# State-space groups of a two-block transformer: decay matrices a chunk ahead, row transposes a group later

## The chip, the core and the metric

The kernel runs on one core of one Trainium2 chip. The metric is the time of one execution in device microseconds. Five engines work side by side and meet at semaphores: TensorE (PE in the rows, its weight loads PEld), VectorE (DVE), ScalarE (ACT), GpSimd (POOL) and SyncE (SP, which here only issues DMAs). Each takes its own instructions in a fixed order.

## The reference, cut to what matters

A sequence of 512 tokens of width 1024 goes through a first block (window attention, indexed attention, cross attention, a feed-forward part) and a second block of two mixers: a state-space mixer and a latent attention. All is float32. The change lies in the state-space mixer alone:

```python
xbc = silu(causal_depthwise_conv(xbc, conv_w, conv_b))      # 4 taps; B, C and x of 8 groups
dt  = softplus(dt_raw + dt_bias);  a = dt * -exp(A_log)     # 32 heads, 4 in a group
# for each group g and each chunk c of 128 tokens:
cb       = C_c @ B_c.T                                      # (t, s)
decay_in = exp(where(causal, acum[t] - acum[s], -inf))      # one matrix for each head
y_diag   = (cb * decay_in) @ (x_c * dt)
y_off    = exp(acum) * (C_c @ state)                        # the state that enters the chunk
state    = exp(acum[-1]) * state + B_c.T @ (decay_to_end * dt * x_c)
y        = y_diag + y_off + D * x
y        = y * silu(z);  y = y * rsqrt(mean(y*y over the group's 256 columns) + eps)
out      = (y * norm_w) @ out_w
```

## The kernel before

Every product of the model is a float32 product made of three matmuls: each operand is split in a rounded part H and a rest L, and `mm3` (L127 to L131) adds H·H, H·L and L·H in PSUM. A weight tile of 128 by 1024 comes by a DMA on SP's queue, ACT makes H from it (L121), POOL makes L (L124). The program is written as plain Python and put in order by a planner: it keeps the order of the source as priority, places each instruction on its engine when its plan says that the inputs are there, and fills in later work where earlier work would wait. The order on each engine is fixed by that plan; on the chip an engine then waits at each instruction for its semaphores.

The state-space part is `block2a`. A PSUM bank holds 128 by 512 numbers; there are eight, three called mm, three px, one py, one po in this part (L1094). For each group g of 8:

- `proj(g, i)`, i = 0 to 3, is a product of 24 matmuls of 512 columns in an mm bank, and `conv` behind it: ACT writes the scaled last tap to `xbc` (L946), DVE adds three taps from PSUM (L948), ACT takes a tanh into the tile `th` (L950), DVE makes silu of both (L951).
- `gate(g, tp)`, tp = 0 and 1, is a product of 48 matmuls of 256 columns in an mm bank, a tanh (L973) and a product (L974).
- `prep(g)` splits B and C, makes C·B for four chunks (L992, px, then `cbm` by L994), transposes B (L997, px) and x (L1004, px twice), and makes `X`, `W` and `y0` (L1011 to L1018).
- `core(g, c)`, c = 0 to 3, has in this order: the decay matrix `Dm` (a DMA from the tensor `acd` issued on ACT's queue, L1028; relu and exp on ACT, L1030 and L1031; times `cbm` on DVE, L1032; split into `M`, L145 and L146), the state's split `E` and its product in po (L1040), the chunk's product in py (L1045 and L1046), the new state's product in px (L1050) and its sum (L1053 to L1056), `y` from py and po (L1062 to L1067), its norm (square on ACT L1070, a scale on DVE L1071, the power -0.5 on POOL L95, a scaled copy on ACT L1073).
- `tr`, one for each chunk, transposes the finished rows of y (L1078, px) and copies or splits them (L1082 to L1091). For g from 4 to 6 a DMA carries them on.

The loop at L1116 runs, for g = 0 to 7: proj 0 and 1 of group g+1, core 0, proj 2 and 3, core 1, gate 1 of group g, core 2, core 3, tr 0, prep of g+1, gate 0 of g+1, tr 1, 2, 3. For g = 7 there is no next group; the output product over Y (L1152) follows, and the planner may draw its first matmuls ahead. `split_first` and `split_second` (L1102 to L1113) make Y from the rows of groups 0 to 3 and 4 to 6.

Of the kernel before, what the change touches and what calls it, by code (L numbers as in the profile page):

```python
# [7 lines left out]
F32 = mybir.dt.float32  # L8
F32R = mybir.dt.float32r
AF = mybir.ActivationFunctionType  # L10
ALU = mybir.AluOpType
# [13 lines left out]
class Net:  # L25
# [891 lines left out]
    def block2a(self, dbg):  # L917
# [25 lines left out]
        def conv(g, i, ps):  # L943
            m = 4 * g + i
            o = gp.tile([P, T], F32, tag="xbc", name=self.nm("xbc"), bufs=5)
            nc.scalar.activation(o, ps, AF.Identity, bias=cb[:, m:m + 1], scale=cw[:, m, 3:4])  # L946
            for j in range(1, 4):
                nc.vector.scalar_tensor_tensor(o[:, j:], ps[:, :T - j], cw[:, m, 3 - j:4 - j], o[:, j:], op0=ALU.mult, op1=ALU.add)  # L948
            th = gp.tile([P, T], F32, tag="th", name=self.nm("th"), bufs=1)
            nc.scalar.activation(th, o, AF.Tanh)  # L950
            nc.vector.scalar_tensor_tensor(o, th, 1.0, o, op0=ALU.add, op1=ALU.mult)  # L951
            G[g]["xbc"].append(o)

        def proj(g, i):
# [23 lines left out]
        def prep(g):  # L978
# [11 lines left out]
            for c in range(NT):  # L990
                q = slice(c * P, (c + 1) * P)
                self.mm3(ps[:, q], BT[0][:, q], BT[1][:, q], CT[0][:, q], CT[1][:, q], c == 0, c == 3)  # L992
            cbm = d["cbm"] = gp.tile([P, NT, P], F32, tag="cbm", name=self.nm("cbm"), bufs=2)
            nc.vector.tensor_tensor(cbm, ps.rearrange("p (c t) -> p c t", t=P), tri.unsqueeze(1).to_broadcast([P, NT, P]), op=ALU.mult)  # L994
            ps = self.bank("px")
            for c in range(3):
# [17 lines left out]
            W = d["W"] = self.pair(gp, [P, 3, 256], "W", bufs=1)  # L1014
            nc.gpsimd.tensor_tensor(v4(xw[:, 0:3, :]), v4(xk[:, 0:3, :]), bc(wde, 3), op=ALU.mult)
            self.split(W[0], W[1], xw[:, 0:3, :])
            y0 = d["y0"] = gp.tile([P, NT, 256], F32, tag="y0", name=self.nm("y0"), bufs=1)
            nc.gpsimd.tensor_tensor(v4(y0), v4(xk), dsk.unsqueeze(1).unsqueeze(3).to_broadcast([P, NT, 4, 64]), op=ALU.mult)  # L1018

        def core(g, c):  # L1020
            d = G[g]
            XX, W, CT, Bt = d["X"], d["W"], d["CT"], d["Bt"]
            hs = slice(4 * g, 4 * g + 4)
            q = slice(c * P, (c + 1) * P)
            ch = lambda v: v[:, c, hs].unsqueeze(2).to_broadcast([P, 4, 64])

            Dm = gp.tile([P, 4, P], F32, tag="Dm", name=self.nm("Dm"), bufs=3)
            nc.scalar.dma_start(Dm, acd[c * 32 + 4 * g:c * 32 + 4 * g + 4, :].partition_broadcast(P))  # L1028
            for h in range(4):
                nc.scalar.activation(Dm[:, h, :], Dm[:, h, :], AF.Relu, bias=acum[:, c, 4 * g + h:4 * g + h + 1], scale=-1.0)  # L1030
            nc.scalar.activation(Dm, Dm, AF.Exp, scale=-1.0)  # L1031
            nc.vector.tensor_tensor(Dm, Dm, d["cbm"][:, c, :].unsqueeze(1).to_broadcast([P, 4, P]), op=ALU.mult)  # L1032
            M = self.pair(gp, [P, 4, P], "M", bufs=2)
            self.split(M[0], M[1], Dm)
            py = self.bank("py")
            if c:
                E = self.pair(gp, [P, 256], "E", bufs=2)
                self.split(E[0], E[1], d["st"])
                po = self.bank("po")[:, :256]
                self.mm3(po, CT[0][:, q], CT[1][:, q], E[0], E[1], True, True)  # L1040

            for h in range(4):
# [3 lines left out]
                nc.tensor.matmul(o[:, 0:64], M[1][:, h, :], XX[:, c, 0, dd], start=False, stop=True, skip_group_check=True)  # L1046

            if c < NT - 1:
                pst = self.bank("px")
                self.mm3(pst[:, :256], Bt[0][:, q], Bt[1][:, q], W[0][:, c, :], W[1][:, c, :], True, True)  # L1050
                sn = gp.tile([P, 256], F32, tag="st", name=self.nm("st"), bufs=2)
                if c == 0:
                    nc.vector.tensor_copy(sn, pst[:, :256])  # L1053
                else:
                    nc.gpsimd.tensor_tensor(w4(sn), w4(d["st"]), ch(dec), op=ALU.mult)
                    nc.vector.tensor_tensor(sn, pst[:, :256], sn, op=ALU.add)  # L1056
                d["st"] = sn

            y = d["y0"][:, c, :]
# [5 lines left out]
                nc.vector.tensor_tensor(w4(yo), w4(po), ch(ea), op=ALU.mult)  # L1065
                nc.gpsimd.tensor_tensor(y, y, yo, op=ALU.add)
            nc.gpsimd.tensor_tensor(y, y, d["zs"][c // 2][:, c % 2, :], op=ALU.mult)  # L1067
            ss = gp.tile([P, 1], F32, tag="gss", name=self.nm("gss"), bufs=4)
            sqj = gp.tile([P, 256], F32, tag="yo", name=self.nm("sqj"), bufs=1)
            nc.scalar.activation(sqj, y, AF.Square, accum_out=ss)  # L1070
            nc.vector.tensor_scalar(ss, ss, 1.0 / 256, 4e-6, op0=ALU.mult, op1=ALU.add)  # L1071
            self.rsq(ss, 1)
            nc.scalar.activation(y, y, AF.Copy, scale=ss)  # L1073

            def tr():
                pt = self.bank("px")
# [14 lines left out]
                    nc.sync.dma_start(dst, ys)  # L1091
            d[f"tr{c}"] = tr

        self.banks(mm=3, px=3, py=1, po=1)  # L1094
        self.ssm_dt(gp, G[0]["zs"], dt, acum, ea, wde, dec, tri, acd)
        for i, ps in enumerate(self.pre):
            conv(0, i, ps)
# [15 lines left out]
                self.split(*Y[k], yT[1][:, k - 8, :], scale=nwg[:, k:k + 1])  # L1113


        for g in range(8):  # L1116
            if g == 7:
                gate(7, 1)
                split_first()
                split_second()  # L1120
            proj(g + 1, 0)
            proj(g + 1, 1)
            core(g, 0)
            proj(g + 1, 2)
            proj(g + 1, 3)
            core(g, 1)
            if g < 7:
                gate(g, 1)
            core(g, 2)
            core(g, 3)  # L1130
            G[g]["tr0"]()
            prep(g + 1)
            gate(g + 1, 0)
            G[g]["tr1"]()
            G[g]["tr2"]()
            G[g]["tr3"]()
        self.flush()
        ctx.close()
        self.Rc = self.rcc.enter_context(self.pool("Rc", "right"))
# [45 lines left out]
    def ssm_dt(self, gp, zs, dt, acum, ea, wde, dec, tri, acd):  # L1185
        nc, a, u = self.nc, self.a, self.u

        scr = gp.tile([P, NT, 256], F32, tag="y0", name=self.nm("dts"), bufs=1).rearrange("p t c -> p (t c)")
        sl = [scr[:, x * P:(x + 1) * P] for x in range(8)]
        t3 = lambda x: x.rearrange("p (t h) -> p t h", h=32)  # L1190
        db, na = sl[7][:, 0:32], sl[7][:, 32:64]
        nc.scalar.dma_start(db, a["ssm_dt_bias"].partition_broadcast(P))
        nc.scalar.dma_start(na, a["ssm_A_log"].partition_broadcast(P))
        bc = lambda v: v.unsqueeze(1).to_broadcast([P, NT, 32])
        nc.scalar.activation(na, na, AF.Exp)
        nc.vector.tensor_scalar_mul(na, na, -1.0)
        v, e, z, z2, q = [t3(x) for x in sl[:5]]
        self.ssm_gate0(gp, v, db, zs)

        nc.vector.scalar_tensor_tensor(e, v, -1.0, v, op0=ALU.mult, op1=ALU.min)  # L1200
        nc.scalar.activation(e, e, AF.Exp)
        nc.vector.tensor_scalar_add(z, e, 2.0)
        nc.vector.reciprocal(z, z)
        nc.vector.tensor_tensor(z, z, e, op=ALU.mult)
        nc.vector.tensor_tensor(z2, z, z, op=ALU.mult)
        nc.vector.tensor_scalar_mul(q, z2, 1.0 / 17)
        for k in range(7, 0, -1):
            nc.vector.scalar_tensor_tensor(q, q, 1.0 / (2 * k + 1), z2, op0=ALU.add, op1=ALU.mult)
        nc.vector.scalar_tensor_tensor(q, q, 1.0, z, op0=ALU.add, op1=ALU.mult)
        nc.vector.tensor_scalar_max(v, v, 0.0)  # L1210
        nc.vector.scalar_tensor_tensor(dt, q, 2.0, v, op0=ALU.mult, op1=ALU.add)
        nc.vector.tensor_tensor(v, dt, bc(na), op=ALU.mult)
        self.defer(lambda: self.ssm_cum(sl, v, dt, acum, ea, wde, dec, tri, acd))
# [410 lines left out]
```

## Time and profile before

| | us |
|---|---|
| median of 3 runs | 1729.89 (1728.51 to 1731.52) |
| the profiled execution | 1732.23 |
| its span, first to last instruction | 1730.5 |

The state-space loop takes the stretch from about 880 to 1222 us of the span. In the profile's rows an engine's busy time is the union of its instructions; a matmul's end is modelled, so idle time of PE is read as a lower bound. "[2.35 <-DVE gss L1071]" behind an instruction says that its engine sat idle for 2.35 us before it, and whose semaphore came last. [...]

### The profile page before, as it was taken

How to read it: one execution, taken by the hardware profiler on the slowest of the kernel's cores; microseconds unless marked ns; L12 is line 12 of the kernel's file. 1: busy time of each engine (PE TensorE's matmuls, PEld its weight loads, DVE VectorE, ACT ScalarE, POOL GpSimd, SP SyncE). 2: the span in 40 equal slices, each digit the busy share in tenths (PEclk: the TensorE clock that was granted, in tenths of full speed). 3: DMA queues.
4: the chain of work that ended last, by engine and by line, in shares of the span. 5: the costliest groups of instructions: out<-in, count | busy, mean ns of one | idle time of the engine just before them, and what ended most of it. 6: DMA issues, size and time to landing. Idle time of an engine off the chain costs nothing.

```text
span 1730.5 us, 27236 instructions
## 1 busy us (share of the span) xinstructions
PE 1663.9 (96%) x10203; PEld 1479.8 (86%) x10203; DVE 927.3 (54%) x1981; ACT 834.1 (48%) x1694; POOL 907.9 (52%) x833
## 2 busy tenths in 40 slices
PE   6999999999999999999999899998999999999998
PEld 6877889889988888887978788888999888989898
DVE  7579763742653014303778877779321306667522
ACT  4455663453443123313557767767433326565532
POOL 6746434353375445544558777777634544344431
PEclk9999999999999999999999999999999999999999
DMA  7634313232232222222332222332324332122341
GB/s 282 196 107 130 106 48 143 95 110 86 86 120 87 97 99 88 95 98 95 125 117 92 86 86 98 110 101 95 146 98 155 130 123 76 52 75 92 110 141 50
DMA packets 68181, 187.23 MB, mean 108 GB/s; under 512 B 9968, under 2 KB 16544, under 8 KB 67792
## 3 DMA queue, kind: packets, MB, share of 16 engines
q1 hardware_dynamic: 50128, 152.95, 26.0%
q10 hardware_dynamic: 17632, 30.43, 5.5%
q8 instruction: 80, 1.31, 0.3%
q0 software_dynamic: 288, 2.10, 0.3%
q14 instruction: 53, 0.43, 0.1%
HBM read 163.86 MB, written 14.78 MB: 103 GB/s over the span
## 4 chain that ended last, share of the span: by engine, by line
PE 71%; DVE 14%; ACT 5%; issue 4%; DMA 3%; POOL 3%; ACTq 0%; DVEq 0%; SPq 0%; POOLq 0%
PE mm L129 12%; PE mm L131 12%; PE mm L130 12%; PE acc L129 5%; PE acc L130 5%; PE acc L131 5%; PE sc L130 2%; PE sc L131 2%; PE sc L129 2%; DMA Dm<-acd 2%; DVE xbc L948 2%; POOL wl L124 2%; PE pv L130 2%; PE pv L131 1%; PE pv L129 1%
## 5 line engine op out<-in xcount | busy, mean ns | idle before, releaser
L124 POOL TENSOR_TENSOR wl<-wraw,wh 128x512 fp32r<-128x512 f32 (+1 forms) x498 | 665.3, 1360 | 515.5 <-ACT wh L121 492.7
L121 ACT ACTIVATE wh<-wraw 128x1024 fp32r<-128x1024 f32 (+4 forms) x254 | 258.3, 1019 | 404.0 <-PE acc L131 123.7
L129 PE MATMUL mm<-xaH,wh 128*128 128x512 f32 x552 | 221.3, 401 | 1.8 <-DVE qbL L140 1.1
L131 PE MATMUL mm<-xaH,wl 128*128 128x512 f32 x552 | 220.8, 400 | 0.0
L130 PE MATMUL mm<-xaL,wh 128*128 128x512 f32 x552 | 220.5, 399 | 0.0
L129 PE MATMUL mm<-wh,xaH 128*128 128x256 f32 x512 | 145.1, 284 | 1.4 <-ACT xaH L145 1.4
L131 PE MATMUL mm<-wh,xaL 128*128 128x256 f32 x512 | 144.6, 284 | 0.9 <-DVE xaL L143 0.9
L130 PE MATMUL mm<-wl,xaH 128*128 128x256 f32 x512 | 144.2, 282 | 0.0
L129 PEld LDWEIGHTS mm<-xaH,wh 128*128 128x128 f32 x552 | 104.9, 190 | 26.1 <-DVE qbL L140 1.5
L131 PEld LDWEIGHTS mm<-xaH,wl 128*128 128x128 f32 x552 | 104.8, 190 | 24.5
L130 PEld LDWEIGHTS mm<-xaL,wh 128*128 128x128 f32 x552 | 104.9, 190 | 23.9
L878 POOL TENSOR_SCALAR S<-S,den 128x128 f32<-128x128 f32 (+1 forms) x96 | 50.9, 534 | 103.2 <-DVE den L877 88.2
L129 PEld LDWEIGHTS mm<-wh,xaH 128*128 128x128 f32 x512 | 96.4, 188 | 2.0 <-ACT xaH L145 1.8
L131 PEld LDWEIGHTS mm<-wh,xaL 128*128 128x128 f32 x512 | 96.2, 188 | 1.2 <-DVE xaL L143 1.1
L131 PE MATMUL mm<-wh,xbL 128*128 128x256 f32 x336 | 94.5, 284 | 2.4 <-DVE xbL L143 2.3
L130 PEld LDWEIGHTS mm<-wl,xaH 128*128 128x128 f32 x512 | 96.4, 188 | 0.2
L129 PE MATMUL mm<-wh,xbH 128*128 128x256 f32 x336 | 95.4, 285 | 0.7 <-DVE lnsum L256 0.5
L130 PE MATMUL mm<-wl,xbH 128*128 128x256 f32 x336 | 94.4, 282 | 0.0
L698 DVE TENSOR_TENSOR rl<-rl 128x512 f32<-128x512 f32 x32 | 43.7, 1365 | 78.5 <-ACT rl L697 78.5
L948 DVE SCALAR_TENSOR_TENSOR xbc<-mm,conv_w,xbc 128x511 f32<-128x511 f32 (+2 forms) x84 | 62.2, 742 | 18.2 <-ACT xbc L946 17.3
L131 PEld LDWEIGHTS mm<-wh,xbL 128*128 128x128 f32 x336 | 63.0, 189 | 3.5 <-DVE xbL L143 2.9
L876 ACT ACTIVATE S<-S,mx 128x128 f32<-128x128 f32 (+1 forms) x96 | 53.7, 560 | 22.6 <-DVE mx L875 20.8
(631 smaller groups left out, 4782.3 us busy)
## 6 DMA issues: line engine op xcount, KB each, us to landing
wraw<-in_w_up SPq DMA_DIRECT2D x32, 512.0 KB, 3.2
wraw<-in_w_down SPq DMA_DIRECT2D x32, 512.0 KB, 3.2
wraw<-in_ssm_xbc SPq DMA_DIRECT2D x32, 512.0 KB, 3.2
Dm<-acd ACTq DMA_DIRECT2D x32, 256.0 KB, 3.3
wraw<-in_ssm_out SPq DMA_DIRECT2D x16, 512.0 KB, 3.5
wraw<-in_mla_z SPq DMA_DIRECT2D x16, 512.0 KB, 3.4
wraw<-in_mla_out SPq DMA_DIRECT2D x16, 512.0 KB, 3.5
wraw<-in_ssm_z SPq DMA_DIRECT2D x14, 512.0 KB, 3.3
```

The costliest lines, as they stand in the source:

```text
L121: nc.scalar.activation(h[:, :n], raw[:, :n], AF.Copy)
L124: (leng or nc.gpsimd).tensor_tensor(l[:, e], raw[:, e], f32(h[:, e]), op=ALU.subtract)
L129: mm(out, aH, bH, start=first, stop=False, skip_group_check=True)
L130: mm(out, aH, bL, start=False, stop=False, skip_group_check=True)
L131: mm(out, aL, bH, start=False, stop=last, skip_group_check=True)
L698: nc.vector.tensor_tensor(r, r, r, op=ALU.mult)
L876: nc.scalar.activation(s, s, AF.Exp, bias=mx, scale=-1.0, accum_out=den)
L878: nc.gpsimd.tensor_scalar(s, s, den, 1.0, op0=ALU.mult, op1=ALU.mult)
L948: nc.vector.scalar_tensor_tensor(o[:, j:], ps[:, :T - j], cw[:, m, 3 - j:4 - j], o[:, j:], op0=ALU.mult, op1=ALU.add)
```

## The change

- `conv`: the tanh is written back into the mm bank that held the product, not into a tile of SBUF; L951 reads it there.
- `core` is cut in two: `decay(g, c)` has the decay matrix up to `M`, and `core(g, c)` the rest. decay 0 of a group is put ahead of proj 0, decay 1 ahead of proj 1, decay 2 behind core 0, decay 3 behind core 1.
- The rows of group g are transposed during group g+1 (two behind proj 0, two behind proj 1), those of group 7 after the loop.
- proj 3 stands between core 2 and core 3; gate 0 of the next group stands ahead of its prep. In group 7 `split_second` stands behind the transposes of group 6.
- py has two banks and px two, not three; the new state's product goes into the second half of the po bank, not into a px bank.
- The norm's scale and power are taken for two chunks at once, behind the odd one.
- `cbm` has one buffer, not two; `y0` has two, not one.

```diff
             nc.scalar.activation(o, ps, AF.Identity, bias=cb[:, m:m + 1], scale=cw[:, m, 3:4])
             ...
-            th = gp.tile([P, T], F32, tag="th", name=self.nm("th"), bufs=1)
-            nc.scalar.activation(th, o, AF.Tanh)
-            nc.vector.scalar_tensor_tensor(o, th, 1.0, o, op0=ALU.add, op1=ALU.mult)
+            nc.scalar.activation(ps, o, AF.Tanh)
+            nc.vector.scalar_tensor_tensor(o, ps, 1.0, o, op0=ALU.add, op1=ALU.mult)
...
-            cbm = d["cbm"] = gp.tile([P, NT, P], F32, tag="cbm", name=self.nm("cbm"), bufs=2)
+            cbm = d["cbm"] = gp.tile([P, NT, P], F32, tag="cbm", name=self.nm("cbm"), bufs=1)
...
-            y0 = d["y0"] = gp.tile([P, NT, 256], F32, tag="y0", name=self.nm("y0"), bufs=1)
+            y0 = d["y0"] = gp.tile([P, NT, 256], F32, tag="y0", name=self.nm("y0"), bufs=2)
...
-        def core(g, c):
+        def decay(g, c):
             d = G[g]
...
-            M = self.pair(gp, [P, 4, P], "M", bufs=2)
+            M = d["M", c] = self.pair(gp, [P, 4, P], "M", bufs=2)
             self.split(M[0], M[1], Dm)
+
+        def core(g, c):
+            d = G[g]
+            XX, W, CT, Bt, M = d["X"], d["W"], d["CT"], d["Bt"], d["M", c]
...
             py = self.bank("py")
+            ob = self.bank("po")
             if c:
                 E = self.pair(gp, [P, 256], "E", bufs=2)
                 self.split(E[0], E[1], d["st"])
-                po = self.bank("po")[:, :256]
+                po = ob[:, :256]
...
             if c < NT - 1:
-                pst = self.bank("px")
-                self.mm3(pst[:, :256], Bt[0][:, q], Bt[1][:, q], W[0][:, c, :], W[1][:, c, :], True, True)
+                pst = ob[:, 256:]
+                self.mm3(pst, Bt[0][:, q], Bt[1][:, q], W[0][:, c, :], W[1][:, c, :], True, True)
...
-            ss = gp.tile([P, 1], F32, tag="gss", name=self.nm("gss"), bufs=4)
+            if c % 2 == 0:
+                d["ss"] = gp.tile([P, 2], F32, tag="gss", name=self.nm("gss"), bufs=4)
+            ss = d["ss"]
             sqj = gp.tile([P, 256], F32, tag="yo", name=self.nm("sqj"), bufs=1)
-            nc.scalar.activation(sqj, y, AF.Square, accum_out=ss)
-            nc.vector.tensor_scalar(ss, ss, 1.0 / 256, 4e-6, op0=ALU.mult, op1=ALU.add)
-            self.rsq(ss, 1)
-            nc.scalar.activation(y, y, AF.Copy, scale=ss)
+            nc.scalar.activation(sqj, y, AF.Square, accum_out=ss[:, c % 2:c % 2 + 1])
+            if c % 2:
+                nc.vector.tensor_scalar(ss, ss, 1.0 / 256, 4e-6, op0=ALU.mult, op1=ALU.add)
+                self.rsq(ss, 2)
+                for i in range(2):
+                    yc = d["y0"][:, c - 1 + i, :]
+                    nc.scalar.activation(yc, yc, AF.Copy, scale=ss[:, i:i + 1])
...
-        self.banks(mm=3, px=3, py=1, po=1)
+        self.banks(mm=3, px=2, py=2, po=1)
...
         for g in range(8):
+            tr = [G[g - 1][f"tr{c}"] for c in range(NT)] if g else [lambda: None] * NT
+            decay(g, 0)
             if g == 7:
                 gate(7, 1)
                 split_first()
+            proj(g + 1, 0)
+            tr[0]()
+            tr[1]()
+            decay(g, 1)
+            proj(g + 1, 1)
+            tr[2]()
+            tr[3]()
+            if g == 7:
                 split_second()
-            proj(g + 1, 0)
-            proj(g + 1, 1)
             core(g, 0)
+            decay(g, 2)
             proj(g + 1, 2)
-            proj(g + 1, 3)
             core(g, 1)
+            decay(g, 3)
             if g < 7:
                 gate(g, 1)
             core(g, 2)
+            proj(g + 1, 3)
             core(g, 3)
-            G[g]["tr0"]()
+            gate(g + 1, 0)
             prep(g + 1)
-            gate(g + 1, 0)
-            G[g]["tr1"]()
-            G[g]["tr2"]()
-            G[g]["tr3"]()
+        for c in range(NT):
+            G[7][f"tr{c}"]()
```

## Rows read from the trace of the kernel before

**Rows 1.** The page's first part: PE's busy time, share of the span, instructions.
```profile
PE 1663.9 (96%) x10203; PEld 1479.8 (86%) x10203; DVE 927.3 (54%) x1981; ACT 834.1 (48%) x1694; POOL 907.9 (52%) x833
```
**Rows 2.** Busy time by stretch, eight groups' stretches: PE, PEld, DVE, ACT, POOL, clock, DMA.
```profile
880.00:923.00 43.00, 40.59 (x227) 33.85 (x226) 32.00 (x52) 31.03 (x72) 25.09 (x22) 1.00 0.32 98
923.00:962.00 39.00, 36.15 (x241) 32.53 (x240) 31.08 (x48) 27.02 (x60) 31.64 (x26) 1.00 0.30 103
962.00:1010.00 48.00, 40.84 (x245) 35.48 (x244) 38.12 (x58) 30.70 (x70) 34.21 (x30) 0.90 0.22 78
1010.00:1050.00 40.00, 40.00 (x261) 35.94 (x261) 33.39 (x55) 31.47 (x68) 32.29 (x27) 0.99 0.32 106
...
1180.00:1222.00 42.00, 36.55 (x297) 35.21 (x296) 36.23 (x53) 25.70 (x52) 26.88 (x24) 1.00 0.20 67
sum 342.00, PE 321.95 PEld 286.13 DVE 273.09 ACT 238.00 POOL 248.62; mean PE 40.24 PEld 35.77 DVE 34.14 ACT 29.75 POOL 31.08
```
**Rows 3.** Waits of PE, 880 to 1222 us: in total, times, longest.
```profile
PE px L1078 <- ACT y L1073: 5.8, 5, 2.0
PE po L130 <- DVE EL L146: 3.0, 4, 1.2
PE po L129 <- DVE yo L1065: 2.9, 3, 1.8
PE py L1045 <- DVE gss L1071: 2.3, 1, 2.3
PE mm L131 <- DVE xbL L143: 2.3, 3, 1.3
PE py L1046 <- DVE ML L146: 1.0, 1, 1.0
```
**Rows 4.** Busy time by stretch as before, two stretches of 10 us.
```profile
970.00:980.00 10.00, 5.62 (x27) 4.21 (x26) 7.84 (x13) 5.90 (x17) 3.89 (x4) 0.84 0.32 106
980.00:990.00 10.00, 10.00 (x59) 8.91 (x58) 9.27 (x13) 8.91 (x19) 9.22 (x7) 0.82 0.23 80
```
**Rows 5.** Timeline from 974 to 979 us: start, length, engine, line, operation.
```profile
974.80 0.30 PE L1045 MATMUL py<-X,MH 128*128 128x128 f32 x1 [2.35 <-DVE gss L1071]
...
976.00 2.45 ACT L1030 ACTIVATE Dm<-Dm,acum 128x128 f32<-128x128 f32 x8 [2.60 <-DMA Dm<-acd]
...
978.90 0.69 PE L1078 MATMUL px<-ident,y 128*128 128x128 f32 x2 [2.04 <-ACT y L1073]
```
**Rows 6.** Timeline from 1007 to 1008 us.
```profile
1007.04 0.15 DVE L1071 TENSOR_SCALAR gss<-gss 128x1 f32<-128x1 f32 x1 [3.56 <-ACT sqj L1070]
...
1007.60 0.58 PE L129 MATMUL po<-EH,CTH 128*128 128x256 f32 x1 [1.76 <-DVE yo L1065]
```
**Rows 7.** Groups by line, 840 to 1230 us: busy us, mean ns | idle us before.
```profile
L1030 ACT ACTIVATE Dm<-Dm,acum 128x128 f32<-128x128 f32 x128 | 41.2, 391 | 23.2 <-DMA Dm<-acd 20.2 <-DVE xd L1011 3.0
L951 DVE SCALAR_TENSOR_TENSOR xbc<-th,xbc 128x512 f32<-128x512 f32 x32 | 31.4, 981 | 12.3 <-ACT th L950 12.3
L95 POOL TENSOR_TENSOR gss<-gss,mhalf 128x1 f32<-128x1 f32 x32 | 21.8, 680 | 37.3 <-DVE gss L1071 37.3
L946 ACT ACTIVATE xbc<-mm,conv_b,conv_w 128x512 f32<-128x512 f32 x28 | 21.4, 764 | 0.0
L950 ACT ACTIVATE th<-xbc 128x512 f32<-128x512 f32 x32 | 20.0, 626 | 25.7 <-DVE xbc L948 25.6
L1071 DVE TENSOR_SCALAR gss<-gss 128x1 f32<-128x1 f32 x32 | 4.7, 146 | 13.3 <-ACT sqj L1070 13.2
```
**Rows 8.** Single lines: ns shortest/median/longest, first and last start, forms.
```profile
L951 DVE SCALAR_TENSOR_TENSOR xbc<-th,xbc x32: 675/778/1807, 851.8 to 1174.5; 128x512 f32<-128x512 f32 x32
L974 DVE SCALAR_TENSOR_TENSOR zs<-zs,mm x14: 670/674/689, 904.4 to 1197.9; 128x512 f32<-128x512 f32 x14
L95 POOL TENSOR_TENSOR css<-css,mhalf x4: 688/692/712, 1354.8 to 1360.1; 128x2 f32<-128x2 f32 x4
```

More of the change, by code (lines that the diff above doesn't have):

```diff
@@ L1016, in prep @@
             self.split(W[0], W[1], xw[:, 0:3, :])
-            y0 = d["y0"] = gp.tile([P, NT, 256], F32, tag="y0", name=self.nm("y0"), bufs=1)
+            y0 = d["y0"] = gp.tile([P, NT, 256], F32, tag="y0", name=self.nm("y0"), bufs=2)
             nc.gpsimd.tensor_tensor(v4(y0), v4(xk), dsk.unsqueeze(1).unsqueeze(3).to_broadcast([P, NT, 4, 64]), op=ALU.mult)
-        def core(g, c):
+        def decay(g, c):
             d = G[g]
[L1022 to L1025, printed above, removed]
             Dm = gp.tile([P, 4, P], F32, tag="Dm", name=self.nm("Dm"), bufs=3)
@@ L1032, in core @@
             nc.vector.tensor_tensor(Dm, Dm, d["cbm"][:, c, :].unsqueeze(1).to_broadcast([P, 4, P]), op=ALU.mult)
-            M = self.pair(gp, [P, 4, P], "M", bufs=2)
+            M = d["M", c] = self.pair(gp, [P, 4, P], "M", bufs=2)
             self.split(M[0], M[1], Dm)
+        def core(g, c):
+            d = G[g]
+            XX, W, CT, Bt, M = d["X"], d["W"], d["CT"], d["Bt"], d["M", c]
+            hs = slice(4 * g, 4 * g + 4)
+            q = slice(c * P, (c + 1) * P)
+            ch = lambda v: v[:, c, hs].unsqueeze(2).to_broadcast([P, 4, 64])
             py = self.bank("py")
+            ob = self.bank("po")
             if c:
@@ L1048, in core @@
             if c < NT - 1:
-                pst = self.bank("px")
-                self.mm3(pst[:, :256], Bt[0][:, q], Bt[1][:, q], W[0][:, c, :], W[1][:, c, :], True, True)
+                pst = ob[:, 256:]
+                self.mm3(pst, Bt[0][:, q], Bt[1][:, q], W[0][:, c, :], W[1][:, c, :], True, True)
                 sn = gp.tile([P, 256], F32, tag="st", name=self.nm("st"), bufs=2)
                 if c == 0:
-                    nc.vector.tensor_copy(sn, pst[:, :256])
+                    nc.vector.tensor_copy(sn, pst)
                 else:
                     nc.gpsimd.tensor_tensor(w4(sn), w4(d["st"]), ch(dec), op=ALU.mult)
-                    nc.vector.tensor_tensor(sn, pst[:, :256], sn, op=ALU.add)
+                    nc.vector.tensor_tensor(sn, pst, sn, op=ALU.add)
                 d["st"] = sn
@@ L1186, in ssm_dt @@
         nc, a, u = self.nc, self.a, self.u
-        scr = gp.tile([P, NT, 256], F32, tag="y0", name=self.nm("dts"), bufs=1).rearrange("p t c -> p (t c)")
+        scr = gp.tile([P, NT, 256], F32, tag="y0", name=self.nm("dts"), bufs=2).rearrange("p t c -> p (t c)")
         sl = [scr[:, x * P:(x + 1) * P] for x in range(8)]
```

## The prediction, made before the change was run

> **What bounds the kernel now.** I read the page's busy shares first, then the busy time of each engine by stretch, then PE's list of waits, then the timeline around the longest of them. The page says that PE is busy for 96% of the span [rows 1], so only what makes PE wait, or what slows its clock, can be won. The change touches the state-space loop. By stretch [rows 2] its 342 us hold 321.95 us of PE time, so PE is idle for 20.05 us: 2.41, 2.85 and 7.16 in the first three groups, 5.45 in the last, and by difference 2.18 in the four between. DVE is the next engine with 273.09 us (80%), then POOL with 248.62 and ACT with 238.00. No other engine is full, but DVE's 38.12 of 48 us in the third group says that it is nearly full for a while. [...]
>
> What ends the idle time of PE is in its list of waits [rows 3]: 5.8 us for the scaled rows of y ahead of the transposes, 3.0 for the split of the state, 2.9 for the po bank to be read, 2.3 for the py product's DVE inputs, 2.3 for the last splits of Y, 1.0 for the decay matrix. The timeline shows how they come about. Around 975 us [rows 5] PE waits 2.35 us ahead of a chunk's product and soon 2.04 us ahead of a transpose; between them ACT stood 2.60 us at a relu whose DMA had not landed, and the scaled copy of y stands behind that relu in ACT's order. [...] Around 1007 us [rows 6] DVE itself stands 3.56 us at the norm's scale (L1071), because ACT's square is late; the read of po behind it in DVE's order is late with it, and PE waits 1.76 us for the bank.
>
> **The change part by part.** The sum is made against the profiled execution, 1732.2 us, and carried over to the median of the three runs, 2.3 us less.
>
> Transposes a group later: each of them now has a gemm and more between it and the copy that it reads. The five waits of 5.8 us [rows 3] lie ahead of 1222 us, where the rows of group 7 are not yet transposed, so they belong to groups 0 to 6; they go, -5.8. Late next is nothing that this wait hid on PE, since the gemm behind it had its weights. The copies behind them move too, and for groups 4 to 6 their DMAs on SP's queue, which stand there between weight loads; SP's queue is never named in PE's waits. For group 6 the copy, its DMA and `split_second` come later, inside group 7; the output product's first matmuls, over groups 0 to 3, cover them, and if they don't, the 2.3 us of waits for these splits [rows 3] grow.
>
> [...]
>
> Norm by pairs: 32 scales and 32 powers become 16. Fewer places where DVE stands for ACT's square: 13.2 us of idle time in 32 [rows 7], so some 6.6 us less of it; the wait that it caused on PE is the 2.9 us for po, of which I take half, -1.45. POOL pays 16 powers of two columns, about 692 ns by the latent part's rows [rows 8], not 32 of 680 [rows 7]: 11.1 for 21.8 us, 10.7 us of POOL, off the path. The even chunk's rows wait for the odd one; their reader is a group later, which covers it, except behind the loop in group 7, where the output product's early matmuls must.
>
> Decay a chunk ahead and py in two banks: the 1.0 us for ML [rows 3] goes, -1.0. Of the 2.3 us [rows 5] I take half, -1.15: two banks free the product from the reading of the one before, but DVE's backlog in that stretch [rows 2] holds the split of X as well. The hoisted steps bring their DMA along: 32 issues and 128 relus on ACT's queue. They stand ahead of conv's and of the weight splits now, so ACT's 20.2 us of standing for landings [rows 7] won't shrink and may double; ACT has 104 of 342 us free [rows 2], and a weight split that is late by 2.6 us [rows 5] is covered by the weight buffers loaded ahead. If that cover fails, PE pays those 2.6 us.
>
> Tanh in PSUM: ACT's write to PSUM has no row here. Nearest are the same tanh to SBUF, 626 ns, and a step that reads PSUM, 764 ns [rows 7]; I take 626, and 140 ns either way are 4.5 us of ACT in 32, off the path. DVE's half is plain: L974, the same kind of operation with one PSUM input, takes 670 to 689 ns, L951 with both in SBUF 675 to 1807 [rows 8], 981 in the mean [rows 7]. So 32 × 0.304 = 9.7 us of DVE go, and with 16 scales of 0.146 us, 2.3 us, together 12.0 of 273 us. None of it lies on PE's path by itself; I count it as zero and as cover for what follows. [...]
>
> What it costs: the mm bank is now held through the tanh and L951, some 0.63 + 0.68 us and a share of the 12.3 us of waits in 32 [rows 7], about 2 us. PE's list names no reader of an mm bank at all, so there is cover of an unknown size. px goes from three banks to two while `prep` takes four of them in a row, each read by ACT or DVE; the new state's product waits for po's reader. The rows show no such wait with three banks, so the cost lies between 0 and a wait of the usual kind at each place (the slower rival has that price); I take 2 us, near the rows that show none.
>
> Sum: 5.8 + 2.4 + 1.45 + 1.0 + 1.15 - 2 = 9.8 us less: 1732.2 - 9.8 = 1722.4 for a profiled execution like this one, 1720.1 by the median; I say 1720.
>
> **The rivals.** *Slower: two px banks.* In `prep` the third and the fourth px bank are first to be freed by `cbm` and by the split of B on DVE, which stand in DVE's order behind whatever is late there, and two decay products with their splits come right behind. PE waits there in order. Seven preps with two such places are 14 waits; the mean of PE's waits for DVE in the second to fourth and the sixth row is 9.2 us in 9, 1.0 us, the longest 2.3 [rows 3]. That is 14 to 32 us, in the middle 23, against 12 won: +11, 1741. From 0.86 us for each place it eats the gain. For it: DVE at 38 of 48 us in a busy group [rows 2]. Against: the planner can lay the next gemm's matmuls between, and DVE loses 12 us of work. [...]
>
> *The order hardly changes.* The source's order is only the planner's priority; it already draws ready work ahead. Then only the transposes and the norms move, and new waits at banks of about 5.8 + 1.45 us take their place: 1729.
>
> [...]
>
> **How the numbers follow.** Forecast 0.50 (its own range 1712 to 1727), slower rival 0.24, no change 0.15, all of it 0.11. The likeliest gives 1720. A measurement can tell about 0.2%, 3.5 us, from no change: below 1726.4 is faster, above 1733.4 slower. Faster is 0.11 and nearly all of the forecast, 0.60; the same 0.16; slower 0.24. The range goes from 1705, where all 25.2 us go, to 1742, just over the middle of the slower rival; some 0.15 lie above it and 0.03 below.
>
> **What would show it.** Right: no wait of PE for L1073 in the loop; L951 at 670 to 690 ns; 16 scales and 16 powers; PE idle near 12 us over the loop and the clock at 1.00 or near it. Wrong: waits of PE at L997, L1004 or L992 for DVE's or ACT's reading of px, the new state's product waiting for L1065, a gemm's first matmul waiting for L951, more ACT time standing for `acd`, or the end of group 7 waiting for the late splits of Y.

## The result and the profile after

The changed kernel takes 1717.55 us (median of 4, 1713.8 to 1718.35) beside 1729.2 us (1727.5 to 1731.52) of the kernel before on the same chip: 11.65 us less by the medians; the ratio of the comparison is 0.9921 with a 95% interval of 0.9905 to 0.9937. The forecast was 1720. Its sign and its size held; most of its terms did not, and the experiments are about that. The profiled execution took 1716.78 us, 0.8 below its median, where that of before lies 2.3 above the median of its runs; so the two traces are 15.45 us apart, and only some 12 us of that is to be explained. Its page begins so:

```profile
span 1714.8 us, 27158 instructions
PE 1657.8 (97%) x10203; PEld 1477.9 (86%) x10203; DVE 913.5 (53%) x1965; ACT 835.6 (49%) x1694; POOL 889.2 (52%) x817
```

Beside [rows 1] the count of matmuls is the same. What changed is how long PE stands. This is the busy time in the loop as a whole, the changed kernel's counterpart of [rows 2]:

```profile
core 0: us, PE busy (x) PEld busy (x) DVE busy (x) ACT busy (x) POOL busy (x), PEclk, DMA share, GB/s
880.00:1206.00 326.00, 318.51 (x2064) 288.12 (x2063) 260.34 (x403) 239.35 (x518) 232.35 (x198) 0.98 0.32 101
```

The loop is 326 us long, not 342, and PE is idle in it for 7.49 us, not 20.05, which is 12.56 us of the difference. The other 3.44 us are busy time of PE, 318.51 for 321.95 us with nearly the same matmuls; their ends are modelled, and I read nothing into it. DVE has 260.34 us of work, not 273.09. PE's clock did not gain. The falls in the loop, added up by slices of 10 us, cost an estimated 1.7 + 1.7 + 0.1 + 1.6 = 5.1 us (the estimate is explained below the slices); the 0.98 of the row above is rounded. The kernel before lost the same, 1.6 + 1.8 [rows 4] + 1.2 + 0.5 = 5.1 us. Here are the slices of the changed kernel, then the two of the kernel before that [rows 4] doesn't show:

```profile
900.00:910.00 10.00, 10.00 (x48) 8.48 (x49) 8.64 (x14) 5.81 (x14) 1.62 (x2) 0.83 0.31 105
930.00:940.00 10.00, 10.00 (x57) 9.23 (x57) 9.60 (x17) 8.10 (x18) 8.24 (x7) 0.83 0.31 89
1170.00:1180.00 10.00, 7.03 (x60) 6.79 (x59) 9.18 (x12) 8.46 (x17) 6.32 (x4) 0.99 0.24 82
1180.00:1190.00 10.00, 10.00 (x74) 10.00 (x74) 9.80 (x14) 8.10 (x16) 5.71 (x4) 0.84 0.10 27
```

```profile
1000.00:1010.00 10.00, 8.06 (x45) 7.08 (x46) 5.24 (x12) 4.35 (x12) 5.25 (x7) 0.88 0.23 80
1010.00:1020.00 10.00, 10.00 (x53) 8.27 (x53) 8.99 (x16) 8.73 (x22) 5.60 (x6) 0.95 0.21 56
```

PEclk is the granted TensorE clock, a mean over the slice. By stretches of 1 us, these falls show 0.50 with 1.00 on both sides, and a number between the two only where the clock steps inside the stretch. So 0.83 over 10 us is 3.4 us at 0.50. Between 900 and 906 us matmuls of 512 columns start 0.43 us apart at 0.50 and 0.23 us apart at 1.00, so I count about half of the time at 0.50 as lost, which is an estimate: each of the first two falls costs 1.7 us, in a stretch in which PE is busy throughout; the idle time lies in the 10 us ahead of it, with PE busy for 7.64 and 8.54 us there.

PE's waits from 830 to 1310 us, which takes in the start of the stage and the output product (columns: line, releaser, us in total, times, longest):

```profile
PE py L1049 <- DVE X L146: 3.0, 1, 3.0
PE px L129 <- DVE dts L1199: 2.8, 1, 2.8
PE po L130 <- DVE EL L146: 2.2, 2, 1.5
PE mm L129 <- DVE xbc L951: 1.2, 1, 1.2
PE po L129 <- ACT WH L145: 1.2, 1, 1.2
PE px L279 <- DVE xcL L146: 0.4, 1, 0.4
PE py L129 <- ACT xcH L145: 0.2, 1, 0.2
```

That is 11.0 us in 8 waits; the kernel before has 21.8 us in 25 over the same window. The difference, 10.8 us, is nearly the 11.65 us of the medians. Of the list before [rows 3] only the split of the state is left; the waits for the scaled rows of y, for the read of po, for the norm's scale, for `ML` and for the last splits of Y are gone.

The groups by line that answer to [rows 7] (mean ns of one behind the busy time, then the idle time ahead of them; L951 is the silu, L950 its tanh, L1028 the decay matrix times `cbm`, L1026 its relu, L1078 the norm's scale, L95 its power):

```profile
L951 DVE SCALAR_TENSOR_TENSOR xbc<-mm,xbc 128x512 f32<-128x512 f32 x28 | 19.2, 685 | 8.8 <-ACT mm L950 8.7
L950 ACT ACTIVATE mm<-xbc 128x512 f32<-128x512 f32 x28 | 16.6, 592 | 12.3 <-DVE xbc L948 12.2
L1028 DVE TENSOR_TENSOR Dm<-Dm,cbm 128x512 f32<-128x512 f32 x32 | 22.4, 724 | 4.0 <-ACT Dm L1027 3.8
L1011 DVE TENSOR_TENSOR xd<-xk,dt 128x512 f32<-128x512 f32 x16 | 20.1, 1261 | 3.3 <-ACT xk L1005 3.3
L1026 ACT ACTIVATE Dm<-Dm,acum 128x128 f32<-128x128 f32 x128 | 41.5, 390 | 13.4 <-DMA Dm<-acd 13.4
L1078 DVE TENSOR_SCALAR gss<-gss 128x2 f32<-128x2 f32 x16 | 6.9, 430 | 7.5 <-ACT sqj L1076 7.5
L95 POOL TENSOR_TENSOR gss<-gss,mhalf 128x2 f32<-128x2 f32 x16 | 13.3, 828 | 10.9 <-DVE gss L1078 10.8
```

### The profile page after: what moved, and what is told of

Same layout as the page of the kernel before. It is cut to its first block, busy times and chain, and to the rows that moved or that the text cites. A ratio compares the mean times of both kernels' runs of the same rounds, so it can differ in the third digit from the quotient of the medians.

```text
span 1714.8 us, 27158 instructions
## 1 busy us (share of the span) xinstructions
PE 1657.8 (97%) x10203; PEld 1477.9 (86%) x10203; DVE 913.5 (53%) x1965; ACT 835.6 (49%) x1694; POOL 889.2 (52%) x817
## 4 chain that ended last, share of the span: by engine, by line
PE 80%; DVE 10%; issue 3%; ACT 3%; DMA 2%; POOL 1%; ACTq 0%; DVEq 0%; SPq 0%; POOLq 0%
PE mm L129 15%; PE mm L131 15%; PE mm L130 15%; PE acc L130 5%; PE acc L131 5%; PE acc L129 5%; PE sc L130 2%; PE sc L131 2%; PE sc L129 2%; PE pv L130 1%; PE pv L131 1%; PE pv L129 1%; PE tr L887 1%; POOL wl L124 1%; DVE sc L479 1%
## 5 line engine op out<-in xcount | busy, mean ns | idle before, releaser
L124 POOL TENSOR_TENSOR wl<-wraw,wh 128x512 fp32r<-128x512 f32 (+1 forms) x498 | 658.0, 1346 | 509.7 <-ACT wh L121 477.4
L129 PE MATMUL mm<-xaH,wh 128*128 128x512 f32 x552 | 221.2, 401 | 3.2 <-DVE qbL L140 1.3
L131 PE MATMUL mm<-xaH,wl 128*128 128x512 f32 x552 | 220.0, 399 | 0.0
L129 PE MATMUL mm<-wh,xaH 128*128 128x256 f32 x512 | 147.2, 288 | 1.4 <-ACT xaH L145 1.4
L131 PE MATMUL mm<-wh,xaL 128*128 128x256 f32 x512 | 145.2, 284 | 0.0
L129 PEld LDWEIGHTS mm<-xaH,wh 128*128 128x128 f32 x552 | 104.4, 189 | 27.2 <-DVE qbL L140 1.8
L131 PEld LDWEIGHTS mm<-xaH,wl 128*128 128x128 f32 x552 | 104.4, 189 | 23.7
L129 PEld LDWEIGHTS mm<-wh,xaH 128*128 128x128 f32 x512 | 97.8, 191 | 2.0 <-ACT xaH L145 1.8
L131 PEld LDWEIGHTS mm<-wh,xaL 128*128 128x128 f32 x512 | 97.0, 190 | 0.1
L129 PE MATMUL mm<-wh,xbH 128*128 128x256 f32 x336 | 94.9, 283 | 0.7 <-DVE lnsum L256 0.5
L131 PE MATMUL mm<-wh,xbL 128*128 128x256 f32 x336 | 94.4, 284 | 0.1
L948 DVE SCALAR_TENSOR_TENSOR xbc<-mm,conv_w,xbc 128x511 f32<-128x511 f32 (+2 forms) x84 | 62.2, 741 | 11.6 <-ACT xbc L946 10.9
L129 PEld LDWEIGHTS mm<-wh,xbH 128*128 128x128 f32 x336 | 63.6, 189 | 1.6 <-DVE lnsum L256 0.7
```

The costliest lines, as they stand in the source:

```text
L124: (leng or nc.gpsimd).tensor_tensor(l[:, e], raw[:, e], f32(h[:, e]), op=ALU.subtract)
L129: mm(out, aH, bH, start=first, stop=False, skip_group_check=True)
L131: mm(out, aL, bH, start=False, stop=last, skip_group_check=True)
```

## The experiments

In each comparison the kernel before ran on the same chip. Times are medians, ratios are against the kernel before with their 95% interval, and "PE waits" is the sum of PE's list of waits from 830 to 1310 us of the profiled execution.

The planner makes a new order for each kernel, so an edit of the source can change much of the order on the engines, or none of it. The traces show which. Take PE's 10203 matmuls in order and compare them, place by place, by the tiles that they write and read. With the tanh alone none differs from the kernel before. With the decay in its own core none differs from the changed kernel, and with the rows in their own group 254 do, all of them at 1185 us or later, in the last of the loop's eight groups. In every other run between 972 and 1942 places differ from the kernel that it is made from. So the two undoings with the same, or nearly the same, order say nothing on what the early decay or the late rows are worth, and the effects of the other runs, but for the tanh alone, hold a new order too.

| kernel | time, before beside it | ratio | PE waits |
|---|---|---|---|
| before | - | 1 | 21.8 in 25 |
| changed | 1717.55, 1729.2 | 0.9921 (0.9905 to 0.9937) | 11.0 in 8 |
| *changed, one part undone* | | | |
| rows in their own group | 1717.32, 1730.52 | 0.9929 (0.9912 to 0.9947) | 9.9 in 7 |
| norm by single chunks | 1722.55, 1730.52 | 0.9953 (0.9936 to 0.9969) | 13.8 in 15 |
| decay in its own core | 1716.33, 1730.52 | 0.9926 (0.9909 to 0.9942) | 10.6 in 8 |
| px three banks, py one | 1712.46, 1730.52 | 0.9903 (0.9887 to 0.9919) | 10.4 in 11 |
| products in old places | 1718.44, 1731.13 | 0.9925 (0.9910 to 0.9940) | 11.3 in 14 |
| rows own group, `y0` single | 1723.45, 1729.22 | 0.9966 (0.9953 to 0.9979) | 14.6 in 15 |
| the same, tanh in SBUF | 1722.52, 1729.22 | 0.9959 (0.9944 to 0.9974) | 13.9 in 17 |
| fourth gate product in py | 1718.51, 1729.22 | 0.9935 (0.9918 to 0.9953) | 12.7 in 14 |
| *before, one part done* | | | |
| norm by pairs | 1736.94, 1731.13 | 1.0037 (1.0024 to 1.0049) | 26.8 in 19 |
| rows a group later, tanh in PSUM | 1722.73, 1731.13 | 0.9954 (0.9939 to 0.9968) | 15.1 in 18 |
| px two banks, py two | 1738.69, 1731.13 | 1.0042 (1.0026 to 1.0059) | 25.6 in 25 |
| tanh in PSUM | 1721.75, 1729.22 | 0.9954 (0.9939 to 0.9969) | 15.2 in 16 |

### Undoing the late rows

```diff
-            tr[0]()
-            tr[1]()
...
-            tr[2]()
-            tr[3]()
...
             prep(g + 1)
+            for c in range(NT):
+                G[g][f"tr{c}"]()
```

> The changed kernel, with the rows of each group transposed at the end of their own group (behind the gate and the prep of the next) and not a group later. My sum: the waits of PE for the scaled copy of y come back, 5.8 us in five, and with them a clock spell of 1.7 to 3.4 us: 6 to 9 us slower than the changed kernel, 3 to 6 us faster than before. Rival, spreading (the gain is the gemms that now stand between the cores): the rows are covered there too, within 2 us of the changed kernel. Rival, DVE time (the gain is DVE's 12 us less): the same as the changed kernel.

The time is the same, 0.9929 beside 0.9921, and no wait for a scaled row came back. But the rows hardly moved: those of groups 0 to 5, and half of group 6, are transposed at the same places of PE's order as in the changed kernel. In the source they stand behind gate 0 and prep of the next group, and the planner lays them as late as in the changed kernel. So this run shows that their late place in the source isn't needed, and does not show what their late place on the chip is worth; the kernel before with late rows (below) bears on that.

### Undoing the norm by pairs

```diff
-            nc.scalar.activation(sqj, y, AF.Square, accum_out=ss[:, c % 2:c % 2 + 1])
-            if c % 2:
...
+            nc.scalar.activation(sqj, y, AF.Square, accum_out=ss)
+            nc.vector.tensor_scalar(ss, ss, 1.0 / 256, 4e-6, op0=ALU.mult, op1=ALU.add)
+            self.rsq(ss, 1)
+            nc.scalar.activation(y, y, AF.Copy, scale=ss)
```

> The changed kernel, with the norm's scale and power for each chunk by itself (32, not 16). My sum: 1.5 us slower than the changed kernel, with DVE standing for ACT's square some 13 us again, not 7.5, and PE waiting for the po bank's read. Rival, spreading: no difference, since a gemm stands behind each core. Rival, DVE time: 2.3 of the 12 us come back, at most 2.3 us slower.

The time is 5.0 us above the changed kernel's median (the two intervals just touch), and PE's waits rise by 2.8 us, in 15 places, not 8. The pairs, with the order that the planner makes for them, are worth some 5 us here, not the 1.45 of the sum.

### Undoing the early decay matrix

```diff
         def core(g, c):
...
+            decay(g, c)
             d = G[g]
...
-            decay(g, 0)
...
```

> The changed kernel, with the decay matrix made at the head of its own core again. My sum: 1 to 2 us slower than the changed kernel, with waits of PE for M. Rival, spreading: the planner's priority for these steps decides how DVE's work lies between the gemms, so without it waits for M come in most groups, over 5 us slower. Rival, DVE time: the same as the changed kernel.

No difference in time (0.9926) or in the waits (10.6 us in 8). There is still no wait for `ML`. But the edit did not reach the chip: the instructions of PE, DVE and POOL stand in the order of the changed kernel, those of ACT too but for one split of a weight. The planner draws the decay ahead by itself, so the run says nothing on what an early decay is worth. Nor did the change make it earlier than before: from the end of a chunk's `ML` to the start of its first product the traces have 12.8 us in the kernel before, in the median of 32 chunks, and 7.2 us in the changed one.

### Undoing the banks

```diff
-        self.banks(mm=3, px=2, py=2, po=1)
+        self.banks(mm=3, px=3, py=1, po=1)
```

> The changed kernel with three px banks and one py bank; the new state's product stays in po's second half. My sum: one py bank costs 1 us, and the 3.0 us wait of PE at the start of the stage (the gate's last product, which waits for the px bank of the product before it to be read) goes with its clock spell of 1.7 us: 2 to 4 us faster than the changed kernel if the rest holds. Rival, py's second bank is what the spread order rests on: PE waits at the py products for the reading of y, 0.4 us or more in most of 32 places, over 8 us slower than the changed kernel.

The lowest median of all, 1712.46 us, 18.1 us under the kernel before beside it. The interval, up to 0.9919, overlaps that of the changed kernel, from 0.9905, so whether it beats that kernel is not settled. What is plain is that the second py bank isn't needed: with one, PE waits for py's reader 2.0 us in two places, and the 2.8 us at the start of the stage are gone. The granted clock of its four executions is 0.991 to 0.993, of the changed kernel's 0.986 to 0.990, and the waits are alike, which points to the clock. It isn't shown: the two profiled executions, at 0.991 and 0.990, lie 3.7 us apart, and of that the clock is worth an estimated 1.7 us, 0.001 of 1715.

### Undoing the places of the products

```diff
             proj(g + 1, 2)
+            proj(g + 1, 3)
...
-            proj(g + 1, 3)
             core(g, 3)
-            gate(g + 1, 0)
             prep(g + 1)
+            gate(g + 1, 0)
```

> The changed kernel with the products in their old places: proj 3 right behind proj 2, no product between core 2 and core 3, the prep ahead of the next gate 0. Undoing the late rows or the early decay cost nothing, so the gain has another bearer. Spreading: 5 to 12 us slower than the changed kernel, with waits of PE for po and py in groups 1 to 6. Rival, norms and DVE time: within 2 us of the changed kernel.

No difference that can be told: 0.9925. With the rows a group later, the old places do as well as the new.

### Pairs alone

The kernel before with the norm's scale and power taken for two chunks, as in the change.

> The kernel before with one edit: the norm's scale and power for two chunks at once. The undo of the pairs cost 4 to 5 us, so if the pairs carry part of the gain by themselves, 3 to 6 us faster than before; my sum had 1.5. Rival: the pairs help only where the rows are read late; here the even chunk's rows, transposed in their own group, now wait for the odd chunk, and PE waits longer for the scaled copy: 0 to 5 us slower than before.

Slower by 5.8 us by the medians; the profiled execution, 1741.9 us, is the slowest of six, so its waits may be more than the usual ones. The timeline around the longest wait shows the way it goes (DVE, then PE; the bracket is the idle time ahead and its releaser):

```profile
929.52 0.42 DVE L1065 TENSOR_TENSOR yo<-po,ea 128x256 f32<-128x256 f32 x1 [2.55 <-ACT sqj L1072]
...
931.37 4.39 DVE L1032 TENSOR_TENSOR Dm<-Dm,cbm 128x512 f32<-128x512 f32 x3
...
940.52 1.66 DVE L146 TENSOR_TENSOR ML<-Dm,MH 128x512 fp32r<-128x512 f32 x1
...
944.17 0.47 PE L1045 MATMUL py<-X,MH 128*128 128x128 f32 x1 [7.14 <-DVE X L146]
```

DVE stands 2.55 us for a square and is then full, also in all of 940 to 950 us in the rows below; the split of `X`, which stands in its order behind three decay products of 4.39 us together, two splits `ML` and others, lets PE wait for 7.14 us. During this wait the clock falls, and it stays low up to nearly 950 us:

```profile
940.00:945.00 5.00, 0.83 (x4) 0.83 (x5) 5.00 (x8) 4.47 (x11) 3.69 (x4) 0.50 0.51 177
945.00:950.00 5.00, 5.00 (x26) 5.00 (x26) 5.00 (x6) 3.14 (x8) 3.34 (x3) 0.53 0.34 113
```

So in the old order the same edit that is worth 5 us in the new one costs about 6. It takes places away at which DVE stands, and lengthens the way from a chunk's square to its rows. That the one counts in the new order and the other in the old is argued and not shown, since the planner's order differs too, in 1442 places of PE.

### Late rows and tanh in PSUM

```diff
+            nc.scalar.activation(ps, o, AF.Tanh)
+            nc.vector.scalar_tensor_tensor(o, ps, 1.0, o, op0=ALU.add, op1=ALU.mult)
...
-            cbm = d["cbm"] = gp.tile([P, NT, P], F32, tag="cbm", name=self.nm("cbm"), bufs=2)
+            cbm = d["cbm"] = gp.tile([P, NT, P], F32, tag="cbm", name=self.nm("cbm"), bufs=1)
...
-            y0 = d["y0"] = gp.tile([P, NT, 256], F32, tag="y0", name=self.nm("y0"), bufs=1)
+            y0 = d["y0"] = gp.tile([P, NT, 256], F32, tag="y0", name=self.nm("y0"), bufs=2)
...
             proj(g + 1, 0)
+            tr[0]()
+            tr[1]()
             proj(g + 1, 1)
+            tr[2]()
+            tr[3]()
```

> The kernel before with the rows a group later, and what makes room for it (tanh in PSUM, one buffer for cbm, two for y0). My sum: 5.8 us of waits and a clock spell go, 6 to 9 us faster than before. Rival: late rows are worth nothing by themselves here either, as the undo said; then what is left is the tanh's DVE time, within 3 us of before.

Faster by 8.4 us. But the tanh alone does the same (below), so the late rows add nothing that can be told.

### Banks alone

```diff
+            ob = self.bank("po")
...
-                pst = self.bank("px")
+                pst = ob[:, 256:]
...
-        self.banks(mm=3, px=3, py=1, po=1)
+        self.banks(mm=3, px=2, py=2, po=1)
```

> The kernel before with the banks of the changed one: px two, py two, the new state's product in po's second half. My sum: 1 us from py, 2 us of new waits, and 3 to 5 us at the start of the stage where the gate's last product waits for a px bank: 2 to 6 us slower than before. Rival, py's second bank carries the gain: 5 us or more faster than before.

Slower by 7.6 us. The waits rise by 3.8 us. New among them are those for `W` at the shared po bank, 5.6 us, and one of 4.5 us behind the loop, in the output product, for an mm bank to be read; why that one comes isn't shown:

```profile
PE mm L129 <- DVE res L755: 4.5, 1, 4.5
PE po L129 <- ACT WH L145: 2.9, 3, 1.3
PE po L130 <- DVE WL L146: 2.7, 4, 1.0
```

The granted clock of its executions is 0.982 to 0.987, where the kernel before beside it has 0.987 to 0.991.

### Tanh in PSUM alone

```diff
-            th = gp.tile([P, T], F32, tag="th", name=self.nm("th"), bufs=1)
-            nc.scalar.activation(th, o, AF.Tanh)
-            nc.vector.scalar_tensor_tensor(o, th, 1.0, o, op0=ALU.add, op1=ALU.mult)
+            nc.scalar.activation(ps, o, AF.Tanh)
+            nc.vector.scalar_tensor_tensor(o, ps, 1.0, o, op0=ALU.add, op1=ALU.mult)
```

> The kernel before with the tanh written into the mm bank, nothing else changed. In the runs so far the rows a group later, the early decay matrix and the place of the products cost nothing when undone alone in the changed kernel, and what all its fast variants keep is the tanh in PSUM and two buffers of y0. Theory A, relief of DVE: L951 at 680 to 690 ns instead of 981 lets DVE, and with it ACT and POOL behind it, run ahead in every group; this edit alone then brings 6 to 9 us, 1721 to 1725, with the waits for the scaled rows shrinking by more than half. Theory B, the prediction on record: DVE's time is off the path and counts zero; then 1729 to 1732, with the waits for the scaled rows of about 5.8 us still there.

1721.75 beside 1729.22 us: 7.5 us less, by two lines. L951 (L950 in this kernel) takes 688 ns, not 981, and PE's waits fall from 21.8 to 15.2 us:

```profile
PE px L1077 <- ACT y L1072: 4.7, 4, 2.4
PE py L1044 <- DVE gss L1070: 2.3, 1, 2.3
PE mm L131 <- DVE xbL L143: 1.9, 3, 1.3
PE po L129 <- DVE yo L1064: 1.2, 1, 1.2
```

The theory of DVE's relief gave the time and missed the place: the waits for the scaled rows were to shrink by more than half, and went only from 5.8 to 4.7 us. What shrank are the small waits for DVE, together from 15.0 to 10.5 us: the state's split, the read of po and others. A better order isn't the cause: PE, ACT and POOL have the same order in both traces, and DVE moves one step at the start of the stage. Nor is it the single buffer of `th`, since ACT's tanh stood for L948 and not for L951 [rows 7]. What is left is time of the engines: by the pages DVE has 10.0 us less (917.3 for 927.3), POOL 9.3 us less (898.6 for 907.9) and ACT 1.1. How the gain divides between DVE and POOL is not told apart.

### The second buffer of y0

The changed kernel with the rows in their own group, as above, and

```diff
-            y0 = d["y0"] = gp.tile([P, NT, 256], F32, tag="y0", name=self.nm("y0"), bufs=2)
+            y0 = d["y0"] = gp.tile([P, NT, 256], F32, tag="y0", name=self.nm("y0"), bufs=1)
...
-        scr = gp.tile([P, NT, 256], F32, tag="y0", name=self.nm("dts"), bufs=2).rearrange("p t c -> p (t c)")
+        scr = gp.tile([P, NT, 256], F32, tag="y0", name=self.nm("dts"), bufs=1).rearrange("p t c -> p (t c)")
```

> The changed kernel with the rows transposed at the end of their own group and one buffer of y0. With two buffers and the rows in their own group the time was that of the changed kernel. If the second buffer is what bears the gain, since the next group's y0 then need not wait for the transposes of this one, 1722 to 1727 and new waits for X, W or y; if it is not, 1715 to 1719.

1723.45 us. With two buffers and the rows in the same place it was 1717.32; the ratios, 0.9966 and 0.9929, have intervals that don't meet. (The scratch `dts` of the stage's start has the buffers of `y0`, and the change gave it two as well.) POOL's product that writes `y0` now stands for the copies and the DMA of the rows that still read the old one:

```profile
L1018 POOL TENSOR_TENSOR y<-xk,dsk 128x1024 f32<-128x1024 f32 x8 | 15.4, 1921 | 6.8 <-ACT xbH L1096 4.4 <-DMA xbL<-y 2.4
```

With two buffers and the rows in the same place the line stands for its input `xk` alone (11.0 us of idle time, all of it). What one buffer costs is not POOL's idle time but the delay: in the eight groups the product starts 0.1 to 1.7 us behind `xk` with two buffers, and 9.9 to 28.9 us behind it with one. So about 6 us of the gain hang on a buffer, with the order that it allows, that the forecast counted as nothing.

### The tanh back in SBUF, on top of that

The kernel of the last section with the `th` tile of the kernel before.

> The changed kernel with the rows transposed at the end of their own group, one buffer of y0, and the tanh in an SBUF tile again: the order of decay matrix and products, pairs and two py banks without the tanh in PSUM. Compared with the same kernel with the tanh in PSUM. Theory A, relief of DVE bears the gain: 5 us or more above that kernel, 1722 to 1727, with L951 near 980 ns and waits for X, the scaled rows or po back. Theory B, the order bears it: within 2 us of that kernel.

1722.52 us, the same as with the tanh in PSUM (0.9959 and 0.9966). The edit that is worth 7.5 us in the old order is worth nothing here, though it costs DVE more than there:

```profile
L951 DVE SCALAR_TENSOR_TENSOR xbc<-th,xbc 128x512 f32<-128x512 f32 x32 | 34.2, 1069 | 5.7 <-ACT th L950 5.5
```

That is 1069 ns a step, not 683, and by the pages DVE has 24.0 us more to do in all (936.3 for 912.3). The order on PE differs in 1595 places, so a new order may have paid for it. It wasn't tried in the changed kernel itself, where the second `y0` takes the room of the tile and of a second `cbm`.

### The fourth gate product in a py bank

```diff
-            ps = self.zpre[t] if t < len(self.zpre) else self.gate0(self.bank("px"), W, t)
+            ps = self.zpre[t] if t < len(self.zpre) else self.gate0(self.bank("px" if t < NT - 1 else "py"), W, t)
```

> The changed kernel with the fourth gate product at the start of the stage in a py bank, not in a px bank. In the changed kernel PE waits 2.8 us there for the third product's bank to be read, since one of the two px banks still holds a convolution's product until its tanh is used, and the clock falls behind it for 1.7 us of loss. If that wait is the price of two px banks, both go: 4 to 4.5 us, 1713. If the wait only moves to the next user of a bank, within 1 us of the changed kernel, 1717.

The wait of 2.8 us is gone, and the time is the same: 0.9935 beside 0.9921. Other waits took its place, with PE's sum at 12.7 us in 14:

```profile
PE py L1049 <- DVE X L146: 2.5, 1, 2.5
PE po L129 <- ACT WH L145: 2.5, 2, 1.6
PE px L1087 <- DVE BtL L146: 2.4, 1, 2.4
PE py L1237 <- DVE dts L1230: 1.5, 1, 1.5
```

The third is a transpose that waits for one of the two px banks to be read. So the price of two px banks is not this one wait.

## Why the forecast held, point by point

**Rows a group later, -5.8.** The waits are gone, as forecast. But the step "late next is nothing that this wait hid" failed. On the kernel before, late rows on top of the tanh cut the waits for scaled rows from 4.7 to 1.1 us, and PE's sum stayed (15.1 for 15.2 us): waits for `X`, the splits of Y, `W` and `xk` came in their place. So in the old order, on top of the tanh, the term measured 0, with some 4 us of uncertainty from the intervals. In the changed kernel it was not measured, since the undoing left the rows where they were.

**Tanh in PSUM, 0.** The durations came out: L951 at 685 ns where 670 to 690 were forecast, 21.9 us in 32 with the four of the stage's start, not 31.4. That is 9.5 us of DVE for the 9.7 of the sum. What failed is "none of it lies on PE's path by itself; I count it as zero". Alone the edit is worth 7.5 us. Most of PE's small waits end at DVE (15.0 of 21.8 us), and with DVE's and POOL's work shorter in an unchanged order several of them shrank.

**Norm by pairs, -1.45.** DVE's standing for the square fell from 13.2 to 7.5 us, close to the 6.6 forecast. The power costs POOL 828 ns, not 692, and the scale costs DVE 430 ns, not the 146 of the sum: 16 of them take 6.9 us, where 32 took 4.7, so the 2.3 us of DVE that the forecast takes off here didn't come. The worth in the changed kernel was mis-sized: some 5 us. That it would cost about 6 alone was not foreseen.

**Decay ahead, -1.0.** The wait for `ML` is gone, but not because the decay comes earlier: `ML` ends 7.2 us ahead of its product, where it had 12.8. The step that failed is that the place in the source decides when the decay is made; the planner draws it ahead from either place. What an early decay is worth was not measured. ACT's standing for `acd` was to stay at 20.2 us or grow; it is 13.4 us.

**py in two banks, -1.15, and the costs, +2.** The wait at py for the norm's scale [rows 5] is gone, also with one py bank. The cost is real: banks alone make the kernel before 7.6 us slower, and the best median is that with three px banks. In the changed kernel it lies between 0 and some 5 us, since the intervals overlap.

**Clock, -2.4.** Failed. No run shows this term: by the estimate above the loop of the changed kernel loses 5.1 us to the clock, and that of the kernel before the same; with the 20.05 us of idle time that comes close to the 25.2 us of the range. Fewer waits did not mean fewer falls: of the eight waits that are left, both of about 3 us and two shorter ones have a fall behind them, each 3.4 us at 0.50, which is 1.7 us by that estimate.

**The sum.** It gave -9.8 and the time moved by -11.65. Its waits were 9.4 us, 7.4 after the costs, and 10.8 us are gone; its 2.4 us of clock did not come, which brings the two totals nearer to each other than their parts are. That they lie 1.85 us apart is in good part luck: the sum had two of the measured bearers at zero, the tanh and the second `y0`. What held is the frame: PE's idle time in the loop, 20.05 us, is what can be won, and 12.56 us of it were; 7.49 us are left, where the forecast had about 12. The single terms don't add up. From the old order the pairs (+5.8) and the banks (+7.6) cost, and the tanh gains 7.5. From the new one the old places of the products can be taken back for nothing; a single `y0` costs some 6 us, and single norms some 5, with intervals that just touch. That is shown. Which parts make the 11.65 us together is not. Why the tanh is worth nothing in the new order stays open: DVE's share of the loop is 80% in both kernels (273.09 of 342 us, 260.34 of 326), so it doesn't show more slack there.

**The slower rival.** Its mechanism is there, at one place in the changed kernel and not at fourteen: 2.8 us at the start of the stage, where the fourth of the gate's products waits for the third's px bank. In `prep`, for which it was worked out, PE's list names no wait at L997 or L1004, and none of the C·B product (its matmuls are named L129 to L131). *The order hardly changes* is right in what it says of the planner, which draws the decay and the rows to the same places without the edits that were to put them there; it fell as a whole with the waits, and the rival by which all of it goes, at 0.11, fell with the 11.0 us that are left.

## What to carry to other kernels

Where PE is 96% busy and its idle time is made of many small waits for the same engine, bound the gain by their sum, and don't credit each wait to the edit that touches it: in two runs here (late rows, the fourth gate product in py) the waits went and others of the same sum, or more, took their place. Work taken off the engine that ends most of those waits can count, though it is on nobody's critical path by itself: 7.5 us in the old order, nothing in the new one. And of a change in parts, ask of each buffer what it lets start earlier: here one more `y0` was worth some 6 us. Where a planner makes the order, compare the order in the two traces before reading an edit's worth from the times: two of the five undoings changed nothing that bears on it.

## What was not expected of the hardware

**With one operand in PSUM, L951 took no longer beside POOL.** With both inputs in SBUF L951 took 675 to 1807 ns in the kernel before; all of the longest ran beside POOL instructions, and the 8 without POOL took 676 to 692. With one input in PSUM the 28 steps of the changed kernel took 675 to 693 ns, 25 of them beside POOL. A longer step beside POOL can also be read in the changed kernel's longest wait, where DVE splits `X` for PE while POOL writes `y0`:

```profile
1172.89 3.20 DVE L1011 TENSOR_TENSOR xd<-xk,dt 128x512 f32<-128x512 f32 x2 [0.26 <-ACT xk L1005]
1176.02 2.38 DVE L146 TENSOR_TENSOR X<-xd,X 128x512 fp32r<-128x512 f32 x1
1172.57 2.97 POOL L124 TENSOR_TENSOR wl<-wraw,wh 128x512 fp32r<-128x512 f32 x2
1175.50 2.34 POOL L1018 TENSOR_TENSOR y<-xk,dsk 128x1024 f32<-128x1024 f32 x1
1178.45 0.33 PE L1049 MATMUL py<-X,MH 128*128 128x128 f32 x1 [2.97 <-DVE X L146]
```

DVE's split is handed over at 1176.02 us, POOL is done at 1177.84, and the split ends at 1178.40, 0.56 us later, where the shortest of the 16 splits of `X` takes 0.68 us in all and this one 2.38. PE waits for it for 2.97 us. The delay moved with the order: the decay product (L1032 before, L1028 now) fell from 1185 to 724 ns in the mean, with 18 of its 32 clear of POOL in the changed kernel and 6 before (673 to 693 ns each in both), while `xd` (L1011) rose from 858 to 1261.

**The tanh took a little less to PSUM than to SBUF:** 592 ns in the mean, 577 to 603, in the changed kernel, where to SBUF it took 626, 612 to 636, in the kernel before. The forecast allowed 140 ns either way.
